# A fused block on one core: the bias table earlier, the last routing tile queued by hand on DVE, three closing sums on POOL

## The chip, the cores and the metric

The kernel runs on one core of a Trainium2 chip. The metric is the device time of one execution in microseconds (us), taken as the median of three. TensorE is called PE here (PEld is its weight load), VectorE DVE, ScalarE ACT, GpSimd POOL, and SyncE, which issues most of the transfers, SP.

## The reference

For 512 tokens of width 1024, in float32, the block computes:

```
proj = x @ w_in                       # one wide projection, cut into chunks
o_a  = softmax-mix of 3 dilated band attentions (4 heads each), bias = rel_bias[bucket(distance)]
o_b  = hgrn2(q, f, i, g):  f = lb + (1-lb)*sigmoid(f_raw); state scan over chunks with cumsum(log f)
o_c  = softmax(q @ k_mem) @ v_mem
merged = sigmoid(g0)*(o_a@w_a) + sigmoid(g1)*(o_b@w_b) + sigmoid(g2)*(o_c@w_c)
x1  = layer_norm(ALPHA*x + merged @ w_out)
gsel = argmax(x1 @ w_rg); two best of the 8 experts of that group, softmax weights * group prob
y   = sum of the two: (silu(x1 @ w_gate[e]) * (x1 @ w_up[e])) @ w_down[e]      # 32 experts
out = layer_norm(ALPHA*x1 + y)
```

## The kernel before, in words

Instructions are written once in program order; a planner puts them into a fixed order for each engine before the run. It takes work that it holds to be ready, earlier written first, so a later step can be pulled ahead into a gap. Inside `tc.manual_schedule(engines=...)` the named engines keep the written order. Each engine runs its queue strictly in order, and pools of tiles are stacks: a pool opened where a closed one lay waits until everything in the closed one has been used for the last time.

Projections are made in chunks of 128 columns. A chunk's weights come by a DMA from SP, ACT casts them to the high part `wh` and DVE subtracts to get the low part `wl` (lines 83 and 84). PE does 24 matmuls of 128x512 into one of two banks called `pj` (line 131); the next chunk but one needs that bank back, and it is given back when ACT has read it.

- **Start, lines 147 to 166.** Ten small matmuls on zeros, then the first chunk (a forget chunk), step by step as the eight slices of x arrive: per slice k ACT makes `xh`, DVE `xl`, and PE does three matmuls.
- **Forget chunks, lines 241 to 268.** For each of 8 heads ACT takes a sigmoid out of the bank (line 244), DVE makes `kfs`, ACT takes a logarithm (line 249) and DVE a running sum. Sigmoid and logarithm lie in different tables of ACT, so a table load stands ahead of each.
- **Memory attention, lines 271 to 307**, with its pool "c", and two gates (line 307).
- **Bias table, lines 311 to 334.** In a pool "a0" of its own, opened behind "c": `tab` holds the 32 rows of `rel_bias`; for each of 5 stretches of 512 columns POOL fetches the one-hot rows `bk` (line 327), ACT casts them to `bkr` (329), PE does one small matmul (331), ACT copies the 12 `rows` out (333), POOL stores them to `bias_d` (334). They are read first when the fifth head of the next stage begins.
- **HGRN heads, lines 343 to 498**, with pool "b" opened behind "a0": `hgrn_front` makes three chunks (q with line 348, vT with line 352, the gate), `hgrn_back` the rest; POOL clears its `batt` and `bq` tiles first (lines 485 and 487).
- **Band attention and merges, lines 506 to 653.**
- **Output product, norm and routing, lines 707 to 787.** For each of four token tiles c: `residual` on DVE (759, 760); `norm_and_route` with the norm (716), transposes by PE, a router product on PE (720), then a chain of small DVE steps (721 to 734), a count on PE (739) and the picks of the first pair of experts (`picked`, line 704); `gain_and_store` multiplies by `l1g` and adds `l1b` (749, 750), on POOL for the first three tiles and on DVE for the last. The pool of `l1g`, `l1b`, `xh` and `xl` (`p1x`) is closed behind it.
- **Experts, lines 794 to 1128.** 16 pairs of experts. On `p1x`'s place ACT clears three `xg` tiles (line 1046, six instructions). The tokens of pairs 0 and 1 are gathered by PE from one-hot picks (line 814) and copied out by ACT and DVE to `xs` (line 826); the others by indirect DMA. `gate_up` (838) and `down` (1054) are the expert's products, `tables` and `overflow_tables` build the index tables on DVE. 192 weight tiles of 512 KB each stream through a ring of 26 buffers on SP (line 114).
- **End, lines 1172 to 1227**, in hand order on DVE and PE. `back[c][0..1]` are the experts' results, read back from DRAM (line 1126). `both(c)` adds the two (1181), `finish(c)` adds on PE, `norm_out(c)` is the last norm: bn_stats (1143), line 1151, ACT line 1158, POOL line 1159; for c = 3 the last step is on DVE (1156). Line 1220 adds `back[3][0]` into x1.

## Time and profile before

| | us |
|---|---|
| median of 3 runs | 1138.49 (1136.7 to 1140.42) |
| the profiled execution's own time | 1141.1 |
| its span, first to last instruction | 1138.7 |
| PE busy in it | 1087.6 (96%) |
| DVE busy | 492.2 (43%) |
| ACT busy | 446.4 (39%) |
| POOL busy | 82.6 (7%) |

Busy times of the engines overlap each other, so they do not add up to the span. [...] The mean granted TensorE clock of the execution was 0.993 of full speed.

### The profile page before, as it was taken

The numbers are of one execution on the slowest core, as the hardware profiler recorded it, in microseconds if no ns is written. First come the engines' busy times: TensorE is split into PE (matmuls) and PEld (weight loads), VectorE is DVE, ScalarE is ACT, GpSimd is POOL, SyncE is SP. The second block draws the span as 40 slices with busy tenths as digits, with TensorE's granted clock in tenths as the row PEclk, the third lists the DMA queues.
The fourth block names the chain that finished last, engine by engine and source line by source line (L and its number), as shares of the span: only waits on it lengthen the run. The fifth ranks groups of instructions, "written<-read, shape, count | busy, mean of one in ns | idle before, by whom it ended". The sixth has DMA issues, their size and how long they took to land.

```text
span 1138.7 us, 17136 instructions
## 1 busy us (share of the span) xinstructions
PE 1087.6 (96%) x6859; PEld 782.2 (69%) x6859; DVE 492.2 (43%) x985; ACT 446.4 (39%) x756; POOL 82.6 (7%) x107
## 2 busy tenths in 40 slices
PE   9999989999999999999999999999999999888884
PEld 6788778778888887887887887888776333332332
DVE  5554467777777323223223223336467111111126
ACT  7965556666666433233233233224114111111112
POOL 1000330000000000000000001000051211110003
PEclk9999999999999999999999999999999999999998
DMA  8742442222222432332331323633956999999992
GB/s 281 235 128 78 119 135 66 83 66 75 83 59 67 117 100 64 103 93 64 103 94 54 96 93 112 216 93 112 382 218 225 378 406 408 400 398 406 408 372 79
DMA packets 70482, 201.22 MB, mean 177 GB/s; under 512 B 16924, under 2 KB 19064, under 8 KB 70400
## 3 DMA queue, kind: packets, MB, share of 16 engines
q1 hardware_dynamic: 63216, 183.92, 46.1%
q0 software_dynamic: 7184, 16.17, 4.1%
q8 instruction: 55, 0.90, 0.3%
q14 instruction: 27, 0.22, 0.1%
HBM read 191.54 MB, written 17.81 MB: 184 GB/s over the span
## 4 chain that ended last, share of the span: by engine, by line
PE 80%; DMA 9%; ACT 6%; DVE 3%; issue 1%; POOL 0%; DVEq 0%; SPq 0%; ACTq 0%; POOLq 0%
PE pj L131 50%; PE pj L838 7%; DMA raw<-in_wexp_dram 7%; PE o L1054 4%; PE tr L222 3%; PE pj L765 2%; PE o L765 2%; ACT wh L83 1%; PE o L570 1%; PE sc L542 1%; PE sc L412 1%; ACT L244 1%; PE sc L548 1%; PE o L304 1%; ACT L249 1%
## 5 line engine op out<-in xcount | busy, mean ns | idle before, releaser
L84 DVE TENSOR_TENSOR wl<-raw,wh 128x1024 fp32r<-128x1024 f32 (+1 forms) x129 | 148.0, 1149 | 253.2 <-PE pj L131 188.3
L83 ACT CAST wh<-raw 128x1024 fp32r<-128x1024 f32 (+1 forms) x137 | 132.6, 969 | 234.5 <-PE pj L131 223.9
L131 PE MATMUL pj<-xh,wh 128*128 128x512 f32 x760 | 203.2, 401 | 3.7 <-ACT bw L352 3.5
L131 PE MATMUL pj<-xl,wh 128*128 128x512 f32 x760 | 196.6, 396 | 0.0
L131 PE MATMUL pj<-xh,wl 128*128 128x512 f32 x760 | 189.9, 392 | 0.0
L131 PEld LDWEIGHTS pj<-xh,wl 128*128 128x128 f32 x760 | 142.7, 188 | 31.1
L131 PEld LDWEIGHTS pj<-xh,wh 128*128 128x128 f32 x760 | 139.9, 189 | 33.4 <-ACT bw L352 3.9
L131 PEld LDWEIGHTS pj<-xl,wh 128*128 128x128 f32 x760 | 142.1, 189 | 29.6
L838 PE MATMUL pj<-raw,xs 128*64 128x512 f32 x432 | 118.5, 599 | 6.4 <-DMA raw<-in_wexp_dram 5.3
L838 PEld LDWEIGHTS pj<-raw,xs 128*64 128x64 f32 x432 | 35.1, 136 | 67.8 <-issue 46.0
L1054 PE MATMUL o<-raw,ehT 128*64 128x512 f32 x204 | 54.2, 617 | 1.2 <-ACT ehT L1064 0.5
L198 ACT ACTIVATE esg<-pj 128x256 f32<-128x256 f32 x16 | 6.2, 384 | 124.5 <-PE pj L838 124.5
L199 DVE SCALAR_TENSOR_TENSOR esg<-esg,pj 128x256 f32<-128x256 f32 x16 | 6.7, 420 | 107.3 <-ACT esg L198 107.3
L609 POOL DMA_DIRECT2D x<-in_xc_dram x4 | 2.1, 538 | 549.1 <-ACT oh L83 549.1
L1114 DVE TENSOR_SCALAR yp<-o,wsl 128x512 f32<-128x512 f32 x14 | 10.5, 750 | 65.5 <-PE o L1054 65.4
L1054 PEld LDWEIGHTS o<-raw,ehT 128*64 128x64 f32 x204 | 16.9, 140 | 28.2 <-issue 22.6
L131 PE MATMUL pj<-oh,wh 128*128 128x512 f32 x128 | 33.8, 393 | 1.4 <-issue 1.4
L131 PE MATMUL pj<-ol,wh 128*128 128x512 f32 x128 | 33.7, 393 | 0.0
L131 PE MATMUL pj<-oh,wl 128*128 128x512 f32 x128 | 33.3, 392 | 0.0
L214 DVE SCALAR_TENSOR_TENSOR sg<-sg,pj 128x512 f32<-128x512 f32 x16 | 11.0, 687 | 42.0 <-PE pj L131 42.0
L131 PEld LDWEIGHTS pj<-oh,wh 128*128 128x128 f32 x128 | 24.0, 188 | 6.5 <-issue 1.4
L131 PEld LDWEIGHTS pj<-oh,wl 128*128 128x128 f32 x128 | 24.0, 188 | 5.2
(399 smaller groups left out, 1460.8 us busy)
## 6 DMA issues: line engine op xcount, KB each, us to landing
raw<-in_wexp_dram SPq DMA_DIRECT2D x159, 512.0 KB, 10.8
raw<-in_w_in_dram SPq DMA_DIRECT2D x95, 512.0 KB, 3.6
wh<-in_wexp_dram SPq DMA_DIRECT2D x18, 512.0 KB, 11.0
wl<-in_wexp_dram SPq DMA_DIRECT2D x15, 512.0 KB, 12.2
yd<-merged SPq DMA_DIRECT2D x8, 512.0 KB, 7.0
raw<-in_w_kv_dram SPq DMA_DIRECT2D x8, 512.0 KB, 3.6
raw<-in_w_bb_dram SPq DMA_DIRECT2D x8, 512.0 KB, 3.6
raw<-in_w_out_dram SPq DMA_DIRECT2D x8, 512.0 KB, 3.7
```

The costliest lines, as they stand in the source:

```text
L83: S.copy(h, src)
L84: (eng or V).tensor_tensor(l, src, h.bitcast(F32), op=OP.subtract)
L131: TE.matmul(acc, wt[:, k * 128:(k + 1) * 128], m[:, k, :], start=n == 0, stop=n == 3 * kt - 1)
L222: TE.transpose(pt[:, j * 128:(j + 1) * 128], src[:, j * 128:(j + 1) * 128], ident)
L244: S.activation(nat(f), cls(acc), AF.Sigmoid)
L249: S.activation(f, f, AF.Ln, scale=oml[:, hd:hd + 1], bias=lb[:, hd:hd + 1])
L304: TE.matmul(o[:, cs], v[:, js], pT[:, js], start=j == 0, stop=j == 1)
L412: TE.matmul(sa4[g * 32:(g + 1) * 32, n, j], X[:, 2 + n, gs], X[:, 2 + n, gs], start=True, stop=True)
L542: TE.matmul(s1[g * 32:(g + 1) * 32, i * 256:(i + 1) * 256], qs[0][:, c * 128 + g * 32:c * 128 + (g + 1) * 32], ks[0][:, lows[g] * 128:lows ...
L765: TE.matmul(acc, m[:, k, cs], w[:, j * 512:(j + 1) * 512], start=k == 0 and n == 0, stop=k == 7 and n == 2)
L838: TE.matmul(acc[rows_, :], xs[:, j * 2 + k, rows_], raws[2 * p + q, j][:, k * 512:(k + 1) * 512], start=j == 0 and k == 0, stop=j == 3 and ...
L1054: TE.matmul(acc[rows_, :], hT[:, k * 128 + q * 64:k * 128 + (q + 1) * 64], raws[2 * p + q, 4 + k][:, n * 512:(n + 1) * 512], start=k == 0, ...
```

## The change

Five edits:

1. At the start, behind the three matmuls of each slice k < 7, PE does two more 128x128 float32 products of a piece of `xl` into a bank nobody reads.
2. The bias table is built right behind the forget chunks, not behind the memory attention. Its small tiles move into the constant pool, `bk` and `rows` into the gates' three `sg` buffers, `bkr` into `obl`, and the pool "a0" is gone.
3. For the last token tile, `residual` and `norm_and_route` keep their written order on DVE, and the gain and the shift of that tile are written in two halves into the chain: half 0 behind the router product, half 1's gain behind line 741, its shift behind the picks.
4. `tc.issue_after(routed.ins)` queues every DVE instruction written from there to the gather of pair 1 (the source of pair 0, the tables, pair 1's picks) behind that last shift.
5. At the end `both(2)`, `both(3)` and the sum of line 1220 go from DVE to POOL, and stand ahead of `hidden`.

```diff
@@ start
+            if k < 7:
+                x0 = xl[:, k, 0:128].bitcast(F32)
+                for j in range(2):
+                    TE.matmul(pt, x0, x0, start=True, stop=True)
@@ behind log_sums (and out of its old place behind sgc)
+    tab = T(cp, [97, 12], tag="tab")
...
+    for j in range(5):
+        w = min(512, 2304 - j * 512)
+        js = slice(j * 512, j * 512 + w)
+        bk = T(gp, [128, 512], tag="sg")[:97]
+        V.memset(bk[32:64, :w], 0.0)
+        for r0 in (0, 64):
+            G.dma_start(bk[r0:r0 + 33, :w], ins["bucket"][:, js])
+        bkr = obl[:97, j, :]
+        S.copy(bkr[:, :w], bk[:, :w])
+        pt = bank("sc")
+        TE.matmul(pt[:12, :w], tabr, bkr[:, :w], start=True, stop=True)
+        rows = T(gp, [128, 512], tag="sg")[:12]
+        S.copy(rows[:, :w], pt[:12, :w])
+        G.dma_start(bias_d[:, js], rows[:, :w])
@@ norm_and_route
+        hs = [slice(j * 512, (j + 1) * 512) for j in range(2)]
...
+        if c == 3:
+            V.tensor_tensor(r[:, hs[0]], r[:, hs[0]], l1g[:, hs[0]], op=OP.mult)
+            V.tensor_tensor(r[:, hs[0]], r[:, hs[0]], l1b[:, hs[0]], op=OP.add)
         V.max(gm[:, c, :], acc[:, 0:8])
...
         S.copy(cums[:, c, :], cum)
+        if c == 3:
+            V.tensor_tensor(r[:, hs[1]], r[:, hs[1]], l1g[:, hs[1]], op=OP.mult)
         picked(c, 0, oh0)
+        if c == 3:
+            return V.tensor_tensor(r[:, hs[1]], r[:, hs[1]], l1b[:, hs[1]], op=OP.add)
@@ gain_and_store
-        for j in range(2):
+        for j in range(2 if c < 3 else 0):
             js = slice(j * 512, (j + 1) * 512)
-            (V if c == 3 else G).tensor_tensor(r[:, js], r[:, js], l1g[:, js], op=OP.mult)
-            (V if c == 3 else G).tensor_tensor(r[:, js], r[:, js], l1b[:, js], op=OP.add)
+            G.tensor_tensor(r[:, js], r[:, js], l1g[:, js], op=OP.mult)
+            G.tensor_tensor(r[:, js], r[:, js], l1b[:, js], op=OP.add)
@@ the loop over token tiles
-        residual(c, 1, acc)
-        norm_and_route(c)
+        if c < 3:
+            residual(c, 1, acc)
+            norm_and_route(c)
+        else:
+            with tc.manual_schedule(engines={mybir.EngineType.DVE}):
+                residual(c, 1, acc)
+                routed = norm_and_route(c)
         gain_and_store(c)
+    behind = ExitStack()
+    behind.enter_context(tc.issue_after(routed.ins))
     p1x.close()
@@ experts, p == 0
             xs = gather(p + 1)
+            if p == 0:
+                behind.close()
@@ end
         def both(c):
-            V.tensor_tensor(back[c][0], back[c][0], back[c][1], op=OP.add)
+            (V if c < 2 else G).tensor_tensor(back[c][0], back[c][0], back[c][1], op=OP.add)
...
         gu = gate_up(15, xs, first)
+        both(2)
+        both(3)
+        G.tensor_tensor(x1[:, 3, :], x1[:, 3, :], back[3][0], op=OP.add)
         sg = hidden(gu)
...
-        both(2)
         finish(1)
         norm_out(accs[1], 1, False)
-        both(3)
-        V.tensor_tensor(x1[:, 3, :], x1[:, 3, :], back[3][0], op=OP.add)
```

## Rows read from the trace of the kernel before

**Rows 1.** The page's part 4: share of the span in the last-ending chain.

```profile
PE 80%; DMA 9%; ACT 6%; DVE 3%; issue 1%; POOL 0%; DVEq 0%; SPq 0%; ACTq 0%; POOLq 0%
```

**Rows 2.** Stretches: length, busy (xcount) of PE, PEld, DVE, ACT, POOL; PEclk; DMA; GB/s.

```profile
14.00:62.00 48.00, 47.36 (x211) 37.90 (x210) 29.20 (x46) 46.77 (x51) 0.00 (x0) 1.00 0.72 239
...
66.00:125.00 59.00, 58.50 (x372) 49.97 (x371) 29.53 (x78) 32.12 (x76) 0.00 (x0) 1.00 0.34 107
...
145.00:150.00 5.00, 1.49 (x7) 0.93 (x6) 3.91 (x9) 3.30 (x4) 4.96 (x9) 0.98 0.26 60
150.00:155.00 5.00, 5.00 (x16) 3.91 (x16) 4.90 (x13) 1.36 (x3) 2.93 (x6) 0.68 0.96 283
...
880.00:890.00 10.00, 9.71 (x45) 3.55 (x42) 4.14 (x15) 1.91 (x4) 2.89 (x5) 1.00 0.84 273
```

**Rows 3.** Timeline (start, us, engine, line, ...) of PE around the first HGRN head.

```profile
143.70 2.00 PE L131 MATMUL pj<-xh,wl 128*128 128x512 f32 x8
149.21 3.29 PE L131 MATMUL pj<-xh,wh 128*128 128x512 f32 x8 [3.51 <-ACT bw L352]
...
156.40 0.60 PE L222 MATMUL tr<-ident,bw 128*128 128x128 f32 x4
```

**Rows 4.** Timeline, POOL's first instruction in pool "b".

```profile
145.04 0.53 POOL L485 MEMSET batt<- 128x512 f32 x1 [0.87 <-DMA biasd<-rows]
```

**Rows 5.** ACT's two lines of the bias table: durations in ns, minimum/median/maximum.

```profile
L329 ACT CAST bkr<-bk x5: 401/615/620, 129.3 to 139.7; 97x512 fp32r<-97x512 f32 x4, 97x256 fp32r<-97x256 f32 x1
...
L333 ACT COPY rows<-sc x5: 364/573/578, 133.9 to 140.4; 12x512 f32<-12x512 f32 x4, 12x256 f32<-12x256 f32 x1
```

**Rows 6.** Timelines of PE and ACT late in the forget chunks.

```profile
52.49 2.00 PE L131 MATMUL pj<-xh,wl 128*128 128x512 f32 x8
...
52.94 1.08 ACT L244 ACTIVATE merged<-pj 128x512 f32<-128x512 f32 x1
...
54.32 1.99 PE L131 MATMUL pj<-xh,wh 128*128 128x512 f32 x8
...
60.39 1.18 PE L131 MATMUL pj<-mmh,wh 128*128 128x256 f32 x8 [0.40 <-ACT merged L244]
```

**Rows 7.** Timeline of PE: the second chunk's start, and small float32 matmuls later.

```profile
15.26 2.12 PE L131 MATMUL pj<-xh,wh 128*128 128x512 f32 x8 [0.20 <-ACT wh L83]
...
849.57 2.70 PE L814 MATMUL o<-oh,x 128*128 128x128 f32 x22
```

**Rows 8.** Timeline from the last token tile's routing to the first expert product.

```profile
855.72 0.17 DVE L721 MAX8 gm<-sc 128x8 f32<-128x8 f32 x1 [0.48 <-PE sc L720]
855.82 0.67 DVE L750 TENSOR_TENSOR x<-x,l1b 128x512 f32<-128x512 f32 x1
...
856.73 1.15 ACT L1046 ACTIVATE xg<-kc 128x512 f32<-128x512 f32 x2 [3.34 <-DVE gi L723]
...
859.20 0.53 DVE L704 TENSOR_SCALAR oh<-kc,cums,memb 128x64 f32<-128x64 f32 x2
...
862.44 7.09 PE L838 MATMUL pj<-raw,xs 128*64 128x512 f32 x32
```

**Rows 9.** Timeline of the end, one POOL product of tile 2, and line 1126's landing.

```profile
842.75 2.50 POOL L749 TENSOR_TENSOR x<-x,l1g 128x512 f32<-128x512 f32 x2 [4.03 <-PE tr L222]
...
DMA to landing us min/median/max: 9.9/10.1/10.2
...
1114.36 1.49 PE L1038 MATMUL tr<-yp,ohs 128*128 128x512 f32 x4
...
1119.84 1.21 DVE L1181 TENSOR_TENSOR raw<-raw,raw 128x1024 f32<-128x1024 f32 x1
...
1121.08 2.17 DVE L1220 TENSOR_TENSOR x<-x,raw 128x1024 f32<-128x1024 f32 x1
1123.18 1.28 DVE L1143 BATCH_NORM_STATS2 lnst<-pj 128x6 f32<-128x512 f32 x2
...
1126.13 1.28 DVE L1143 BATCH_NORM_STATS2 lnst<-o 128x6 f32<-128x512 f32 x2
```

## The prediction

> **What bounds the kernel now.** I read first the chain that ended last: PE holds 80% of it, DMA 9%, DVE 3% [rows 1], so an edit is worth what it does to PE, except in two places: the last 25 us, a DVE chain, and a middle part where the weight stream sets the pace. Then the stretches. From 14 to 62 us PE is busy 47.36 of 48 us, and ACT 46.77 of 48: two full engines. From 66 to 125 ACT has half its time free (32.12 of 59). From 145 to 150 PE is busy only 1.49 of 5 us, and from 150 to 155 its granted clock is 0.68 [rows 2]: that is the one hole in the first 800 us. Last the timelines around each edit.

> **Edit 2, what it takes away.** PE ends the second chunk of head 0 at 145.5 and starts the next at 149.21, after 3.51 us without work; these 24 matmuls then take until 156.40 [rows 3]. In steady flow eight starts lie 54.32 - 52.49 = 1.83 us apart [rows 6], so 24 take 5.5 us, not 7.2: the other 1.7 us is the clock of 0.68 behind the hole [rows 2]. The hole comes from the bias table. POOL's first clearing in pool "b" starts at 145.04, after waiting for the last store of `rows` [rows 4]: "b" lies where "a0" lay, so q's and v's tiles, and ACT's copy that gives the `pj` bank back, waited for that store. With "a0" gone, "b" follows "c", done near 127. The five table matmuls leave too; at 0.229 us for 512 columns (half for the last) 4.5 x 0.24 = 1.1 us. So that chunk starts at 145.5 - 1.1 = 144.4 and ends at 149.9 instead of 156.4: **-6.5 us**. Nothing else is late there: the weights' cast has its buffer by then, and q's two steps fall due five us earlier than the bank.

> **Edit 2, what it adds.** The 1.1 us of PE go where PE is full. On ACT come 4 x 0.615 + 0.40 + 4 x 0.573 + 0.364 = 5.5 us and two casts of `tab`, some 5.9 us [rows 5]. They meet a full engine: sigmoid 6 leaves ACT at 54.02, and the chunk that needs its bank starts at 54.32; at 60.39 PE already waits 0.40 us for a sigmoid [rows 6]. So what the planner puts on ACT between 15 and 60 us delays PE one for one, past the 1.2 us that ACT idles there (48 - 46.77), and PE's 1.1 us vanish into that wait: at most 5.9 - 1.2 = +4.7. At least +1.1, if the copies fall ahead of 14 us or behind 62. The code stands behind all forget chunks and the planner takes what is ready, so I expect a mixture: **+3.0**, about the middle. The one-hot rows are fetched by POOL beside the x slices, 10 x 67 KB; at the 239 GB/s of that stretch [rows 2] the first three pairs cost 1.7 us of transfer; most would wait behind nothing that PE needs, I take +0.2 with 0 and +1.5 as ends. DVE's small steps have room (29.20 of 48) [rows 2].

> **Edit 1.** 14 products as two matmuls each: 22 such matmuls span 2.70 us [rows 7], 0.115 each, so 28 are 3.2 us. Up to slice 5 PE waits for x and they fill that; behind slices 5 and 6, which come in a rush, 8 x 0.115 = 0.9 us would push the second chunk past 15.26, whose start already waited on ACT [rows 7]. ACT then rules until 62, so part of it is lost in slack: **+0.2**, ends 0 and +0.9. A gain would need a low clock early; the granted clock was 1.00 in 14 to 62 [rows 2] and the hole shows what a low one looks like.

> **Edits 3 and 4.** They shorten a DVE chain: from the router product's end at 855.72 to the end of the last picks at 859.73 it is 4.0 us, with a 0.67 us shift in between [rows 8] and picks of pair 1. Without these it is nearer 3.0, also after the 0.69 us gain of half 1 is written in. But PE is not waiting for it. It runs the 64 matmuls that gather pair 0 (a piece is in rows 7) and 20 of the 64 for pair 1 meanwhile, and the product of pair 0 starts at 862.44 without a gap on PE. Holding pair 1's picks behind the chain takes that filling away. So no gain can come from here unless PE's work shrinks, and it doesn't. Costs: 14 of these 20 stood ahead of the last picks, 14 x 0.115 = 1.6 us; the picks come 1.0 us earlier, so PE runs dry for about 0.6 us. Then ACT: its six clearings, 0.57 us each, began only after the last use of `l1b` (855.82 + 0.67, start 856.73) [rows 8]. That last use is now behind the picks, near 859.5. The clearings are written ahead of the copy of `xs`; if the planner issues them first, the copy ends at 859.7 + 3.4 + 0.6 = 863.7, and the expert product starts 1.3 us later, with PE dry for some 2.9 us less what pair 1's gather fills. The ends are 0 and 0.6 + 2.9 = +3.5; I take **+0.9**, near the end where PE has other work at hand. It carries to the end one for one: from 880 to 890 the stream runs at 273 GB/s because it waits for PE to free buffers [rows 2], so the later DMA-bound stretch starts by as much later.

> **Edit 5.** The end is a DVE chain. The bn_stats of tile 2 starts at 1123.18 and that of tile 3 at 1126.13; ahead of them stand two sums of 1.2 us and one of 2.17 us on DVE [rows 9]. Without the three: PE ends tile 1 at 1114.36 + 1.49 = 1115.85, tile 1's norm takes DVE 3.05 us to 1119.0, tile 2's 2.95 us to 1122.0; PE's own order for tiles 2 and 3 (12 more products for each) ends near 1118.7 and 1122.3. So tile 3's bn_stats starts at 1122.3, not 1126.13: **-3.8**. POOL must be in time: it does 512 columns in 1.25 us [rows 9], so each sum of 1024 takes 2.5; `back[2]` lands near 1108, `back[3]` at 1101.4 + 9.9 = 1111.4 [rows 9]; sums end at 1110.5, 1114.0 and 1116.5, and PE wants the last near 1119.6. Cover gone means the sums took 3.6 us each: then 1118.6, still in time. Behind nothing on POOL queues anything until tile 0's line 1159 at 1116.7.

> DVE's 2.17 us for a sum that took 1.21 at 1119.84 ran beside a POOL sum [rows 9]. [...] The row shows a stretch of 1.0 us, which PE's order hides.

> **Sum.** -6.5 + 3.0 + 0.2 + 0.2 + 0.9 - 3.8 = -6.0 us. The profiled execution took 1141.1 us, 2.6 above the median of the runs, so it would be 1135.1 there; against the median of 1138.49 it is **1132.5 us**.

> **Rivals.**
> (a) *Forecast*: the mixture above, chance 0.50, 1132.5; its own range is 1129 to 1135.5.
> (b) *The copies find free places on ACT* (ahead of 14 us or behind 62, where it idles 45%): +1.1 instead of +3.0, and nothing for the middle: 1132.5 - 1.9 - 0.9 = 1129.7. For it: 32.12 of 59 in rows 2. Against: the code stands earlier and nothing holds it back. Chance 0.20.
> (c) *Full price everywhere*: +4.7, +1.5, +0.9 and +3.5 against -10.3: 1138.8, no change. For it: ACT's 46.77 of 48 and the clearings' place. Against: PE has other work in the middle. Chance 0.17. Here too if the end's sums come late and only half of 3.8 remains.
> (d) *Slower*: ACT stands still in the forget chunks. A bias copy whose one-hot rows have not landed stops the sigmoids behind it, PE's banks stay taken, and the clock falls as it did at 150. Five copies that each wait some 2.5 us behind the full queues, with 5.9 us of work and one fall of the clock (1.7): 12.5 + 5.9 + 1.7 - 1.2 = +18.9 instead of +3.0: 1148.4. It decides from where this place costs more than 3.0 + 6.0 + 3.4 = 12.4 us. Against: the rows land long before ACT is through with the first heads if POOL fetches early. Chance 0.07.
> (e) *The change doesn't do what it says*: the table is planned behind the memory attention again, "b" is not free earlier: -6.5 and +3.0 fall away, 1132.5 + 3.5 = 1136.0, chance 0.06.

> **From this the numbers.** A median differs from no change here if it is off by more than about 0.3%, 3.4 us: below 1135.1 is faster, above 1141.9 slower. Faster: 0.45 of (a), all of (b), 0.01 of (e): 0.66. Same: 0.05 of (a), 0.15 of (c), 0.05 of (e): 0.25. Slower: 0.07 of (d) and 0.02 of (c): 0.09. The range takes in (b) with its lower side and (c): 1127 to 1139.5; outside are (d) and the tails, some 0.18.

> **What would show it.** In the changed profile: PE busy nearly 5 of 5 us in the stretches that answer to 145 to 155, at a granted clock of 1.00 (edit 2); between 14 and 62 PE waits for ACT at lines 244 or 83, 2 to 4 us in all, and ACT's bias copies stand among the sigmoids; ACT's copy to `xs` stands behind six clearings, and the first expert product comes 0 to 3.5 us later against the end of the output product; tile 3's bn_stats starts 3 to 4 us nearer to tile 0's, with DVE going from tile to tile without a sum. The prediction is wrong if PE's waits ahead of 62 us exceed 6 us, if a hole near the first HGRN head remains, or if PE at the last tile waits for POOL.

## The result, and the profile after

The changed kernel took 1152.26 us (median of 4 runs, 1151.76 to 1153.04) against 1138.04 for the kernel before beside it: a ratio of 1.0125, 95% interval 1.0109 to 1.014, or some 14 us slower. Forecast were 1132.5, with 1127.0 to 1139.5 as the range. Of the rivals only (d) was slower than the kernel before, at 1148.4, for a stop of ACT in the forget chunks that did not come.

Stretches of the kernel after, columns as in [rows 2]:

```profile
14.00:62.00 48.00, 47.42 (x202) 37.58 (x203) 29.75 (x49) 46.45 (x55) 0.00 (x0) 1.00 0.74 245
66.00:125.00 59.00, 56.86 (x358) 49.25 (x359) 29.20 (x67) 33.59 (x74) 10.96 (x21) 0.97 0.47 141
145.00:150.00 5.00, 5.00 (x23) 4.03 (x22) 3.89 (x7) 1.55 (x3) 0.00 (x0) 1.00 0.33 86
150.00:155.00 5.00, 5.00 (x23) 4.07 (x22) 2.34 (x5) 2.30 (x3) 0.00 (x0) 1.00 0.24 95
875.00:880.00 5.00, 5.00 (x18) 1.44 (x16) 3.44 (x22) 0.97 (x3) 0.00 (x0) 0.66 0.37 125
```

The hole at 145 to 155 is closed, as forecast, and in the forget chunks (14 to 62) PE is as busy as before. But PE is short of 2.1 us at 66 to 125, where it had been short of 0.5 [rows 2], the granted clock there is 0.97 in the mean, and a new fall of the clock lies at 875. What PE waits for, from the list of waits (us in total, times, longest; "issue" stands where the profile shows nothing that PE waited for) of the kernel after:

```profile
PE pj L857 <- ACT xs L845: 3.8, 6, 2.4
PE sc L419 <- issue: 3.0, 2, 1.7
PE sc L294 <- ACT ol L292: 2.6, 2, 2.2
PE sc L422 <- issue: 1.4, 1, 1.4
PE sc L415 <- issue: 0.9, 1, 0.9
PE sc L320 <- ACT cp L326: 0.9, 1, 0.9
```

and the same list of the kernel before has of these kinds only

```profile
PE pj L838 <- ACT xs L826: 1.4, 5, 0.3
PE pj L131 <- issue: 1.4, 1, 1.4
PE sc L412 <- issue: 1.2, 1, 1.2
PE sc L291 <- ACT cp L297: 0.5, 1, 0.5
```

By these waits the kernel after loses some 8 us. Against them stand the gains, the wait of 3.51 us in the hole that is closed [rows 3] and the shorter end below, so a good part of the 14 us is in no wait. PE's timeline of the kernel after, in steady flow:

```profile
24.37 2.02 PE L131 MATMUL pj<-xl,wh 128*128 128x512 f32 x8
26.23 2.03 PE L131 MATMUL pj<-xh,wl 128*128 128x512 f32 x8
```

Eight starts lie 1.86 us apart, in the kernel before 1.83 [rows 6], at a granted clock of 1.00 in both. The kernel does 3 x 760 + 3 x 128 = 2664 such matmuls (the counts of line 131); at 0.03 / 8 us each, that is some 10 us.

The middle and the end, from ACT's, PE's, DVE's and POOL's timelines of the kernel after:

```profile
870.66 3.23 ACT L1065 ACTIVATE xg<-kc 128x512 f32<-128x512 f32 x6 [1.43 <-DVE x L755]
873.79 0.56 ACT L845 COPY xs<-o 128x512 f32<-128x512 f32 x1
...
1123.94 2.36 POOL L1202 TENSOR_TENSOR raw<-raw,raw 128x1024 f32<-128x1024 f32 x1 [33.87 <-DMA raw<-in_ln_dram]
...
1124.78 2.61 DVE L1202 TENSOR_TENSOR raw<-raw,raw 128x1024 f32<-128x1024 f32 x1
...
1128.73 1.29 DVE L1164 BATCH_NORM_STATS2 lnst<-sc 128x6 f32<-128x512 f32 x2 [0.68 <-PE sc L1057]
...
1137.61 1.29 DVE L1164 BATCH_NORM_STATS2 lnst<-o 128x6 f32<-128x512 f32 x2
```

and tile 0's bn_stats in the kernel before:

```profile
1112.78 1.30 DVE L1143 BATCH_NORM_STATS2 lnst<-sc 128x6 f32<-128x512 f32 x2 [2.08 <-PE sc L1038]
```

ACT does the six clearings ahead of the copy to `xs`. At the end DVE goes from tile 0's bn_stats to tile 3's in 8.88 us; in the kernel before it took 13.35 us [rows 9].

### The profile page after: what moved, and what is told of

The parts are those of the page before. It is cut to its first block, busy times and chain, and to the rows that moved or that the text cites. A ratio compares the mean times of both kernels' runs of the same rounds, so it can differ in the third digit from the quotient of the medians.

```text
span 1150.2 us, 17183 instructions
## 1 busy us (share of the span) xinstructions
PE 1098.5 (96%) x6887; PEld 787.8 (68%) x6887; DVE 490.6 (43%) x982; ACT 446.7 (39%) x756; POOL 88.8 (8%) x110
## 4 chain that ended last, share of the span: by engine, by line
PE 80%; DMA 7%; issue 7%; DVE 2%; ACT 2%; POOL 0%; DVEq 0%; ACTq 0%; POOLq 0%; SPq 0%
PE pj L131 50%; PE pj L857 8%; DMA raw<-in_wexp_dram 6%; PE o L1073 4%; PE tr L226 3%; PE o L777 2%; PE pj L777 2%; PE o L573 1%; PE sc L545 1%; PE sc L415 1%; PE sc L551 1%; PE o L333 1%; PE sc L725 1%; PE o L581 1%; PE o L454 1%
## 5 line engine op out<-in xcount | busy, mean ns | idle before, releaser
L131 PE MATMUL pj<-xh,wh 128*128 128x512 f32 x760 | 205.1, 402 | 0.2
L131 PE MATMUL pj<-xl,wh 128*128 128x512 f32 x760 | 197.7, 397 | 0.0
L131 PE MATMUL pj<-xh,wl 128*128 128x512 f32 x760 | 192.5, 395 | 0.0
L131 PEld LDWEIGHTS pj<-xh,wl 128*128 128x128 f32 x760 | 142.9, 188 | 33.5
L131 PEld LDWEIGHTS pj<-xl,wh 128*128 128x128 f32 x760 | 142.1, 188 | 31.9
L131 PEld LDWEIGHTS pj<-xh,wh 128*128 128x128 f32 x760 | 139.7, 189 | 30.9 <-ACT wh L83 1.3
L131 PE MATMUL pj<-oh,wh 128*128 128x512 f32 x128 | 34.4, 398 | 0.0
L131 PE MATMUL pj<-ol,wh 128*128 128x512 f32 x128 | 34.1, 396 | 0.0
L131 PE MATMUL pj<-oh,wl 128*128 128x512 f32 x128 | 33.8, 395 | 0.0
L131 PEld LDWEIGHTS pj<-oh,wl 128*128 128x128 f32 x128 | 24.1, 188 | 5.7
L131 PEld LDWEIGHTS pj<-ol,wh 128*128 128x128 f32 x128 | 23.9, 188 | 5.5
```

The source lines that it names most:

```text
L131: TE.matmul(acc, wt[:, k * 128:(k + 1) * 128], m[:, k, :], start=n == 0, stop=n == 3 * kt - 1)
```

## The experiments

### Where the tiles lie

The three small tiles of edit 2 take 64 bytes each in the constant pool; `raw`, `wh`, `wl` and what follows lie 192 bytes further, while `xh`, `xl`, `oh` and `ol`, allocated from the other side, stay. Theory A: this is the loss that shows in no wait. (The stationary tile of a matmul is the second operand of its call in the kernel, here a piece of `wh` or `wl`; the moving tile is the third, here `xh` or `xl`.)

**shift192**: the kernel before with an unused tile.

```diff
+    T(cp, [128, 48], tag="pad")
     wp = es.enter_context(tc.tile_pool(name="wp", bufs=3))
```

> The kernel before with one unused tile of 192 bytes in the constants, so that the weight tiles raw, wh and wl (and what is allocated after them on that side) lie 192 bytes further, where the changed kernel has them; nothing else differs. Theory A (most of the loss is the place of the stationary tiles): the L131 matmuls of 128x512 lie 0.232 us apart instead of 0.229, so some 2660 of them cost 8 us: 1146 us, 1144 to 1148. Theory B (the spacing grew for a reason in the change's own work): 0.229 us and 1138 us, within 0.3% of the kernel before.

1147.4 us, ratio 1.0078 (1.0059 to 1.0097). The starts in its timeline lie 1.86 us apart:

```profile
30.27 2.02 PE L132 MATMUL pj<-xh,wl 128*128 128x512 f32 x8
32.13 2.02 PE L132 MATMUL pj<-xh,wh 128*128 128x512 f32 x8
```

**after_noshift**: the changed kernel, its small tiles in space that is there.

```diff
-    tab = T(cp, [97, 12], tag="tab")
+    tab = T(gp, [128, 512], tag="sg")[:97, :12]
...
-    tabr, tabh = (T(cp, [97, 12], F32R, tag=t) for t in ("tabr", "tabh"))
+    tabr, tabh = (obl[:97, n, 0:12] for n in (6, 7))
```

> The changed kernel with its three small table tiles placed in space that it has anyway (a gate buffer and two unused slices of the low-part tile), so that every tile that both kernels have lies where it lay before; the instructions are the same. Theory A: 0.229 us between the L131 matmuls again and 1144 us, 1142 to 1146: still slower than before by the middle and the start. Theory B: 0.232 us and 1152 us as the changed kernel.

1143.8 us, 1.004 (1.0026 to 1.0055), and the starts lie 1.83 us apart again:

```profile
31.00 1.99 PE L131 MATMUL pj<-xh,wl 128*128 128x512 f32 x8
32.83 1.99 PE L131 MATMUL pj<-xh,wh 128*128 128x512 f32 x8
```

Theory A holds from both sides: an unused tile costs 8 to 9 us, and the same instructions without the shift give them back.

**addr_map**: added groups of 24 matmuls, the operand's start moved by 32 bytes from group to group.

```diff
+    b = bank("sc")
+    for n in range(24): TE.matmul(b, stb[:, 8 + n % 2 * 128:136 + n % 2 * 128], xh[:, n % 8, :], start=n == 0, stop=n == 23)
...
```

> The kernel before with 32 added groups of 24 matmuls of 128x512 each behind the forget chunks (their results are not used): in 16 groups the stationary starts at 16 places 32 bytes apart, in 16 groups the moving operand does. Theory A: the time of a group of 24 falls into at least two levels by the stationary's place, some 0.229 and 0.232 us apiece (5.50 and 5.57 us a group). Theory B: one level for all 16. Both: the whole is some 180 us longer.

One run, with the granted clock at 1.00 in all groups; only its groups are compared with each other. By line (busy us, mean ns of one), lines 280 to 310 move the stationary tile, 312 to 342 the moving one:

```profile
L284 PE MATMUL sc<-xh,stb 128*128 128x512 f32 x24 | 5.7, 392 | 0.0
...
L288 PE MATMUL sc<-xh,stb 128*128 128x512 f32 x24 | 5.6, 389 | 0.0
...
L304 PE MATMUL sc<-xh,stb 128*128 128x512 f32 x24 | 5.6, 389 | 0.0
...
L312 PE MATMUL sc<-mvb,stb 128*128 128x512 f32 x24 | 5.6, 390 | 0.0
L314 PE MATMUL sc<-mvb,stb 128*128 128x512 f32 x24 | 5.8, 395 | 0.0
L316 PE MATMUL sc<-mvb,stb 128*128 128x512 f32 x24 | 5.7, 392 | 0.0
```

In this run there are three levels, and they repeat every 256 bytes. By the addresses in the built program `stb` and `mvb` start at byte 96 of 256, `xh` at 224. With moving minus stationary as the distance modulo 256, it is 0 on lines 288, 304, 312 and 328 (389, 390 ns) and 64 on 284, 300, 316 and 332 (392); all the others, 128 on 280 and 32 on 314 among them, have 394 to 396. So in this run not the stationary's place alone counts, but the distance. In the kernel before `wh` lies at 160, a distance of 64; in the kernel after at 96, a distance of 128. Neither is the best, which asks for

**align64**: 64 bytes more, `wh` and `wl` at 224 like all four moving tiles.

```diff
+    T(cp, [128, 16], tag="pad")
```

> The kernel before with an unused tile of 64 bytes in the constants: raw, wh and wl lie 64 bytes further, which puts the stationary wh and wl and the moving xh, xl, oh, ol at the same place modulo 256 bytes. Theory A1 (from the map of places: what counts is the distance between moving and stationary tile modulo 256 bytes, equal is best): 128x512 matmuls of L131 0.2275 us apart instead of 0.229, so 2660 of them give back 4 to 8 us: 1131 to 1135 us, faster than before. Theory A2 (what counts is the stationary's place by itself, as 160 of 256 is good and 96 bad): no gain, 1138 us or slower.

1131.54 us, 0.994 (0.9919 to 0.9962): faster than the kernel before by an unused tile. Its timeline has 1.81 us for eight:

```profile
28.28 1.98 PE L132 MATMUL pj<-xl,wh 128*128 128x512 f32 x8
30.09 1.98 PE L132 MATMUL pj<-xh,wl 128*128 128x512 f32 x8
```

### Each part alone

Each is the hunks of the change's own diff on the kernel before, without the shift.

**start_alone** (edit 1):

```diff
+            if k < 7:
...
+                for j in range(2):
+                    TE.matmul(pt, x0, x0, start=True, stop=True)
```

> The kernel before with edit 1 alone, the 14 filler matmuls between the x slices. Theory C (the stalls of PE named issue in the bursts of small matmuls move with the number of PE instructions ahead of them): the two stalls of before (1.4 and 1.2 us) are replaced by others, more or fewer, and the time goes with their sum, 1137 to 1141 us. Rival: the stalls belong to edit 2's instructions and stay at 1.4 and 1.2 us; the fillers cost 0 to 1 us at the start: 1138 to 1139 us.

1142.61 us, 1.0031 (1.0014 to 1.0049), above the 1137 to 1141 expected. The memory attention begins at 59.47 us (before at 60.39 [rows 6]); that tells little, as kernels whose start is as before begin it between 59.80 (order_late_clear) and 63.12 (middle_alone). But the stalls named issue are four now, 5.6 us against 2.6:

```profile
PE sc L420 <- issue: 2.5, 2, 1.8
PE sc L423 <- issue: 1.8, 1, 1.8
PE sc L416 <- issue: 1.3, 1, 1.3
```

**bias_alone** (edit 2, the small tiles placed as in after_noshift):

```diff
+    for j in range(5):
+        bk = T(gp, [128, 512], tag="sg")[:97]
...
-    with tc.tile_pool(name="a0", bufs=2, side="right") as tp:
```

> The kernel before with edit 2 alone, the three small table tiles in space that it has anyway, so that no tile lies elsewhere. Theory: the hole of 4 us at 145 to 155 goes, PE's waits at 62 to 87 give 3 to 4 us back: at the first burst of small matmuls (174 us) 1 to 2 us are won, and the time is 1135 to 1138 us with the two issue stalls as before, up to 3 us more with four. Rival (forecast): 6.5 us go and 3 come: 1134 us. Rival (the loss of the changed kernel without the shift lies here): 1141 us or more.

1138.54 us, 0.9998 (0.9987 to 1.001): nothing, where the theory had 1135 to 1138 and the forecast's terms 1134. The hole at 145 to 155 is gone, but its waits are

```profile
PE sc L290 <- ACT ol L288: 3.6, 2, 2.7
...
PE sc L316 <- ACT cp L322: 1.0, 1, 1.0
```

and the clock falls behind the first of them, as it did behind the hole. A stretch of the columns of [rows 2], and eight matmuls of 128x256 ahead of the wait and behind it:

```profile
65.00:70.00 5.00, 4.35 (x25) 4.25 (x26) 2.94 (x3) 2.61 (x6) 1.03 (x2) 0.66 0.57 191
...
60.40 1.08 PE L131 MATMUL pj<-mmh,wh 128*128 128x256 f32 x8
...
66.69 1.91 PE L131 MATMUL pj<-mmh,wh 128*128 128x256 f32 x8
```

The eight take 1.08 us at a clock of 1.00 and 1.91 here; in the kernel before the clock from 65 to 70 is 1.00. So a hole of the old kind came back 80 us earlier.

**middle_alone** (edits 3 and 4):

```diff
+            with tc.manual_schedule(engines={mybir.EngineType.DVE}):
+                residual(c, 1, acc)
+                routed = norm_and_route(c)
...
+    behind.enter_context(tc.issue_after(routed.ins))
```

> The kernel before with edits 3 and 4 alone, the order written for DVE from the last tile's residual and the queueing behind it. Theory D (the loss of 4.5 us between residual(3) and pair 15 is theirs): PE dry 2.4 us ahead of gate_up(0) for the xs copy behind six clearings on ACT, the granted clock below 1 in that product, the weight stream starved behind it: 1143 us, 1141 to 1144. Rival (the place came from what the other edits shifted ahead of it): 1138 to 1139 us, dry 0.5 us at most.

1144.63 us, 1.0049 (1.0034 to 1.0064). PE is dry for 2.40 us ahead of `gate_up(0)`, and the product takes 8.62 us instead of 7.09 [rows 8], as the clock falls behind the wait:

```profile
865.77 4.75 PE L854 MATMUL pj<-raw,xs 128*64 128x512 f32 x14 [2.40 <-ACT xs L842]
...
865.00:870.00 5.00, 4.23 (x14) 1.35 (x16) 4.79 (x27) 2.31 (x5) 0.00 (x0) 0.66 0.01 3
```

From the first gather matmul to tile 0's bn_stats at the end the trace has 267.3 us, against 261.6 to 263.2 in before, start_alone, bias_alone and end_alone: the loss lies there.

**end_alone** (edit 5):

```diff
-            V.tensor_tensor(back[c][0], back[c][0], back[c][1], op=OP.add)
+            (V if c < 2 else G).tensor_tensor(back[c][0], back[c][0], back[c][1], op=OP.add)
```

> The kernel before with edit 5 alone (the sums of the second pair's picks and the last tile's own sum on POOL, queued behind pair 15's gate and up). By the trace after, the end from pair 15's last gate to the last DVE step shrank by 4.5 us and nothing else is touched: 1133.6 us, 1132 to 1135. Rival: the end only shrank because the other edits brought that stage in with less behind it: 1137 to 1139 us.

1135.17 us, 0.9968 (0.9958 to 0.9978), with tile 3's bn_stats at 1121.62, 8.88 us behind tile 0's as in the kernel after.

In per cent the shift and the four parts are +0.78 +0.31 -0.02 +0.49 -0.32 = +1.24, and the whole change measured +1.25: the parts add up. That they do so within 0.01 is luck; the five intervals taken together allow some 0.3 either way.

### The stalls named issue

**warm24**: as many added matmuls as in edit 1 (14 products, 28 matmuls in the trace), but where PE waits for the first data.

```diff
-    for j in range(10):
-        TE.matmul(pt, idle, idle, start=True, stop=True)
+    for j in range(24):
+        TE.matmul(pt[:, :48], idle, idle[:, :48], start=True, stop=True)
```

> The kernel before with 24 idle matmuls of 48 columns at the start in place of 10 of 128 columns: 14 matmuls more on PE, as edit 1 adds, at a place where PE waits for the first data anyway; they leave no work out. Theory C (the issue stalls depend on the number of PE instructions ahead): the stalls of edit 1 alone come back at the same instructions (four in the bursts of small matmuls, 5 to 6 us in sum instead of 2.6) and the time is 2 to 3.5 us above before: 1141 to 1142.5 us. Rival (they came from the fillers' place between the x slices, through what runs earlier or later behind it): the two stalls of 1.4 and 1.2 us stay, 1138 to 1139 us.

1145.9 us, 1.0059 (1.0039 to 1.0078), above the 1141 to 1142.5 expected. The four stalls of start_alone come back at the same instructions (its lines are 4 lower), 4.8 us in sum, 2.2 more than before. The memory attention begins at 63.37, 3 us later than before, which kernels with an unchanged start do too (63.12 in middle_alone); the rest of the 7 us stays open, so the time itself proves less than the list:

```profile
PE sc L416 <- issue: 2.6, 2, 1.6
PE sc L419 <- issue: 1.8, 1, 1.8
PE sc L412 <- issue: 0.4, 1, 0.4
```

**fillers7**: edit 1 with half the fillers.

```diff
-                for j in range(2):
+                for j in range(1):
```

> Edit 1 alone with one filler between the slices instead of two, 7 matmuls instead of 14. Theory C (the issue stalls in the bursts of small matmuls depend on how many PE instructions lie ahead): number, places or sum differ both from before (two, 2.6 us) and from edit 1 (four, 5.6 us); the time is before's plus the difference of the sums, less up to 0.9 us won at the start. Rival (any filler at the start costs through the clock or the data there): stalls as in one of the two, time between 1138 and 1143 us without relation to their sum.

1139.76 us, 1.0013 (1.0002 to 1.0024), stalls of 1.8, 1.7 and 0.4 us: 3.9 in sum, between the two, as is the time. What follows the number of PE instructions ahead is the place. Stretches from the start to each stall, first of before, then of start_alone (the count behind PE's busy time is its matmuls so far):

```profile
0.00:227.10 227.10, 218.23 (x1614) 178.34 (x1615) 138.47 (x294) 151.75 (x252) 21.19 (x44) 0.99 0.44 141
0.00:252.90 252.90, 242.57 (x1870) 198.43 (x1870) 158.21 (x338) 168.28 (x282) 21.19 (x44) 0.99 0.42 134
...
0.00:222.20 222.20, 215.97 (x1616) 179.89 (x1616) 137.15 (x289) 149.99 (x248) 21.25 (x44) 1.00 0.45 143
0.00:282.40 282.40, 274.19 (x2254) 227.71 (x2254) 180.65 (x388) 187.50 (x318) 21.25 (x44) 1.00 0.40 129
```

The first stall comes behind the same 1614 to 1616 matmuls in both, whatever these are, and the others lie 256 and 638 behind it. In five kernels (before, start_alone, warm24, fillers7 and the kernel after) every stall of 0.3 us or more that is named issue lies at 1615 + 128 n matmuls, within 4: n is 0 and 2 in before, 0, 5, 10 and 12 in start_alone, warm24 and the kernel after, 0, 5 and 10 in fillers7. So in these five the places are fixed in PE's count, at multiples of 128 matmuls with their 128 weight loads, and added matmuls move other code onto them; how much is lost differs with the code there (n = 5: 1.78 us in start_alone, 0.37 in fillers7), and for n = 0 it is 1.36 to 1.80 us. The queue list of the kernel before shows 55 packets of instructions, 0.90 MB, 16 KB each; over its 6859 matmuls and as many weight loads that is 249 to a packet, near the 256 of one step of n. In this kernel one such packet moves in the microsecond from 224, the stall is 225.86 to 227.22, and the next moves from 228; likewise 250, 251.81 to 252.97, 254. The places and this coincidence in time are what the traces show; what PE waits for there was not shown. Two such stalls stand in the kernel before, with 2.6 us, and four in the one after, with 5.3.

### The middle

**order_alone**: middle_alone without edit 4.

```diff
-    behind.enter_context(tc.issue_after(routed.ins))
...
```

> Edit 3 alone: the order written for DVE from the last tile's residual, without the queueing of tables and picks behind it (edit 4). Theory D1 (edit 4 delays the clearings of xg on ACT until DVE's last step, and they then stand ahead of the xs copy): without it the clearings run at 856 to 860 us again, gate_up(0) waits 0.5 us at most at full clock, 1139 to 1140 us. Theory D2 (the order on DVE itself, with the last tile's gain put between the routing steps, is what delays): PE dry 2 us and more, 1143 to 1145 us as with both.

1143.24 us, 1.0043 (1.0029 to 1.0058). My theory D1 fell: without edit 4 the same six clearings still wait for DVE's last shift, and PE is as dry (here the clock stayed at 1.00 behind it):

```profile
859.80 3.23 ACT L1060 ACTIVATE xg<-kc 128x512 f32<-128x512 f32 x6 [1.43 <-DVE x L752]
...
863.55 7.09 PE L852 MATMUL pj<-raw,xs 128*64 128x512 f32 x32 [2.40 <-ACT xs L840]
```

`xg0` and `xg1` lie where `l1g` and `l1b` lay, so the clearings wait for the last step that reads these. Edit 3 puts it behind the picks. What edit 4 adds, 0.49 against 0.43%, is not clear of the noise.

**order_late_clear**: the clearings written behind the gather of pair 0.

```diff
         xgs.append(T(mp, [128, 1024], tag=f"xg{j}", bufs=1))
+    xs = gather(0)
+    for j in range(AHEAD):
         for h in range(2):
             S.mul(xgs[j][:, h * 512:(h + 1) * 512], i512, 0.0)
-    xs = gather(0)
```

> Edit 3 alone with the clearings of the three xg tiles issued behind the xs copies of pair 0 instead of ahead of them. Theory E (xg lies where the gains l1g and l1b lay, so the clearings wait for the last step that reads them, which edit 3 puts 4 us later, and stand ahead of the xs copy on ACT): PE's wait for xs falls from 2.40 to 0.5 us or less and gate_up(0) begins 2 us earlier; 1141 us, 1139.5 to 1142, 2 us below edit 3 alone. Rival (the xs copy waits for the picks' own selectors, behind the routing steps on DVE): the wait stays at 2 us, 1143 us.

1140.75 us, 1.0016 (1.0003 to 1.0029), and the wait is gone:

```profile
859.74 0.57 ACT L840 COPY xs<-o 128x512 f32<-128x512 f32 x1
...
860.48 7.09 PE L852 MATMUL pj<-raw,xs 128*64 128x512 f32 x32
```

Theory E holds. Though the product now begins 10.9 us behind the first 22 gather matmuls, which start at 849.57 in both kernels, where the kernel before took 12.9 [rows 7, 8], nothing is won in the whole: all 64 matmuls of pair 1's picks stand behind the product, and 20 of them, some 2.3 us, stood ahead of it before.

### The bias table

**bias_buckets_first**: edit 2 with bucket tiles of their own, fetched ahead of the loop.

```diff
+    bks = [T(bp, [97, 512 if j < 4 else 256], tag=f"bk{j}") for j in range(5)]
...
-        bk = T(gp, [128, 512], tag="sg")[:97]
```

> Edit 2 alone with five bucket tiles of their own, fetched ahead of the loop, and only the row tiles in the gate buffers. Theory F (in edit 2 each bucket transfer stands behind the row transfer before it on POOL and waits for a gate buffer, so PE waits 3.6 us for ol and 1.0 us for cp at 62 to 87 us, and a forget product waits for its table): these waits go to 1 us at most and 3 to 4 us are won: 1135 us, 1134 to 1136.5. Rival (what counts is ACT, full in the forget chunks, and the table work costs there what the hole gave): 1138 to 1139 us, ACT's waits only lie elsewhere.

1145.44 us, 1.0059 (1.0044 to 1.0073): theory F fell, and so did its rival of 1138 to 1139. The buckets are there, the small matmuls move ahead of the last forget sigmoids, and then PE stands for ACT, which is busy 45.72 of 47 us from 15 to 62:

```profile
61.42 1.07 PE L294 MATMUL sc<-ol 97*12 97x512 f32 x2 [5.17 <-ACT sg L296]
65.27 0.39 PE L294 MATMUL sc<-ol 97*12 97x256 f32 x1 [2.77 <-ACT ol L292]
```

As far as these two runs show, what the table costs is ACT's time, wherever its data come from; the slow hand-over through the gate buffers had kept it out of the fullest stretch.

### Better than both

**align_end**: align64 and edit 5. **align_end_bias**: edit 2 too. **align_end_bias2**: with bias_buckets_first.

```diff
+    T(cp, [128, 16], tag="pad")
...
+            (V if c < 2 else G).tensor_tensor(back[c][0], back[c][0], back[c][1], op=OP.add)
```

> The kernel before with the unused tile of 64 bytes (the weight tiles at the same place modulo 256 bytes as the moving operands) and edit 5 alone. The two gains lie in different stages (the products up to 850 us, the end behind 1102 us) and add: -7.5 and -4.1 us, 1127.5 us, 1126 to 1129, faster than both kernels. Rival (the end's gain depends on what came before it): 1130 to 1132 us.

> The same with edit 2 too, its small tiles in space that is there. By the run of edit 2 alone (no difference, 1138.5 against 1139.1 us) 1127 us, 1125.5 to 1129, no difference from the kernel without it that can be told. Rival (edit 2's gain was eaten by its own stalls of issue and with other places comes out): 1124 to 1125 us.

> The better places (64 bytes), edit 5, and edit 2 with bucket tiles of their own. Theory F: 1125 us, 1123.5 to 1126.5, faster than the same with edit 2 as it was (1128.6). Rival: 1128 to 1129 us.

1128.86 us, 0.9912 (0.9892 to 0.9932); 1128.59, 0.9912 (0.9897 to 0.9926); 1134.2, 0.9955 (0.9942 to 0.9967). The first two beat both kernels, by some 10 and 23 us; the two gains add, and edit 2 adds nothing. The third missed its range of 1123.5 to 1126.5, and its rival too, with theory F.

## Why the prediction was wrong, point by point

The sum was -6.0 us and the measured change some +14. The largest step that failed is one that the sum did not have, the place of the tiles; three of its terms were too small besides. None of the three signs that were to show it wrong came: from 14 to 62 us PE is idle for 0.6 us, no hole is left near the first HGRN head, and PE does not wait for POOL at the last tile. They looked only where the sum had terms.

- **A term that the sum did not have: +8.9 us** (0.78% of 1139). Edit 2 was read for its instructions, buffers and waits; that its tiles in the constant pool move every weight tile was in the diff, and I took "its small tiles move into the constant pool" for free.
- **Edit 1, +0.2 taken, +3.5 measured** (1.6 to 5.6). At the start no cost of the fillers can be told, as the step says. What can be found of the loss, 3.0 us, lies 200 us later, in the stalls named issue. No row of mine asked what PE's stalls named issue in [rows 1] hang on.
- **Edit 2, -6.5 + 3.0 + 0.2 taken, -0.2 measured.** The hole went, as worked out, at a clock of 1.00. The ACT term was right in kind and too small, +6.1 instead of +3.0, and in another place: the forget chunks were spared, the table stretched to 87 us, and PE waited there 3.6 + 1.0 us in bias_alone and then lost some 1.3 us more at a clock of 0.66 (an estimate from its starts between 66 and 69.5). That the clock falls behind such a wait was priced for the hole that went, and not for the one that came. bias_buckets_first shows the price in the forget chunks that rival (d) feared, +0.59% in place of -0.02%: some 7 us, not the 12 it needed.
- **Edits 3 and 4, +0.9 taken, +5.6 measured**, above the end of +3.5. The mechanism stood in the step: the clearings wait for `l1b`, stand ahead of `xs`, and PE runs dry for up to 2.9 us (it was 2.40). I took the end where PE has other work; pair 1's picks, that work, were what the change held back: in middle_alone the product of pair 0 begins 13.4 us behind the first gather matmul, 0.5 later than before, with the 2.3 us of 20 of pair 1's matmuls still to do. The clock's fall that follows (0.66 at 875 to 880 in the kernel after, 1.5 us in the product of middle_alone) was not in the sum. That makes 4.3 of the 5.6; the rest is within the interval. Of order_alone's +0.43%, order_late_clear removes 0.27.
- **Edit 5, -3.8 taken, -3.6 measured.** In the trace tile 3's bn_stats stands 4.5 us nearer to tile 0's. Beside POOL's sum DVE's `both(1)` took 2.61 us instead of the 1.21 of such a sum in [rows 9] and ended 1.1 us after it. That stretch of 1.4 us was hidden by PE's order: in end_alone `both(1)` took 2.67 us, and tile 0's bn_stats still starts at 1112.74, before at 1112.78.

## What to carry to other kernels

Before a tile is added to a pool, look at what it moves: compare the matmuls' start-to-start spacing and the operands' places modulo 256 bytes, and try one unused tile as padding. A step that is first in its queue on another engine (a clearing that waits for reused space) must be followed when its last reader is moved. When matmuls are added or taken away, look whether stalls named issue moved into other code. An unexplained difference is best split by running each part alone: here five parts summed to the whole within their intervals.
